# The recurrence's small levels on four column groups of TensorE, with compact diagonal blocks

## The chip, the cores and the metric

The kernel runs on one core of a Trainium2 chip. The metric is the device time of one execution in microseconds; the time before is the median of three runs.

## The reference

One layer of a streaming encoder for 1024 prompt tokens and 64 sample tokens (T = 1088), model width 1024, in fp32. One input projection feeds eight heads of forgetting attention and four heads (128 wide) of a gated linear recurrence, both gated, joined, and mapped by one output projection. The part that matters here is the recurrence, S_t = diag(f_t) S_{t-1} + k_t v_t^T, o_t = S_t^T q_t, in chunks:

```python
b = jnp.cumsum(logf, axis=1)
o_inter = jnp.einsum('blhk,bhkv->blhv', q * jnp.exp(b), S0)
diff = b[:, :, None] - b[:, None, :]
decay = jnp.exp(jnp.where(causal[None, :, :, None, None], diff, -jnp.inf))
A = jnp.einsum('bthk,btshk,bshk->bhts', q, decay, k)
o = o_inter + jnp.einsum('bhts,bshv->bthv', A, v)
b_last = b[:, -1]
S_new = jnp.exp(b_last)[..., None] * S0 + jnp.einsum('bshk,bshv->bhkv', jnp.exp(b_last[:, None] - b) * k, v)
```

The decay sits inside the sum over k, so A is no plain product of q and k.

## The kernel before

The work falls into four stages: loading and splitting x and the weights, with the projection of the attention's values; the attention with the projections of its keys and queries as filler; from about 340 us on the recurrence, whose four heads are interleaved with the remaining projections and with the first half of the output projection; and the rest of the output projection with the final norm, from about 640 us on.

Projections are split in three fp32r products (high by high, low by high, high by low). `t_block` (L248) gives 128 output columns for 364, 364 and 360 tokens, 24 matmuls each, into one of two `pj` banks of PSUM; DVE and ACT read the bank out (L1060, L1061 and the like).

**A head of the recurrence** (`hgrn_head`, L1092 on) computes A without cumulative sums, in a binary tree over chunks of 128 tokens (`NT` = 8, and the 64 sample tokens as a ninth). At level b a block of 2b tokens has an upper half of keys and a lower half of queries; the keys k are scaled up to the block's middle and the queries q from there, and their product is the block's b x b corner of A. `update(b)` then scales k, q1 and the products of forget values F on DVE for the next level. Level 0 is the diagonal (a sum over k by a product with `ones`, L1146 and L1147). Levels 1 and 2 share one product (queries copied to `qx`), levels 4 and 8 another (copied to `qy`, where level 8 takes two masks). Up to level 16 a product takes all 128 keys of a chunk as the stationary side and the lower-half queries of the chunk as the moving side (`pe.matmul(out, stationary, moving)`): L1166, L1227 and, through `level_mm`, L1105. Only a few small blocks of each 128-row result are wanted. `copy_predicated` on DVE puts these into `AT` (128 keys x 9 chunks x 128 queries) under the constant `masks`. The sample's products are half as large and go to a bank of their own (`psm`: L1147, L1179, L1239, L1108), with masked copies of their own (L1119, L1180, L1182, L1241).

Level 32 already uses 32 keys as the stationary side (L1260), with the outputs of a chunk's two halves on PSUM partitions 0 to 31 and 64 to 95, hence two column groups of 32. Level 64 uses 64 keys, all outputs on partitions 0 to 63 (L1273, copied to AT by L1275). Then k is transposed to `kn` (L1287), the states S of the chunks are made (L1306, L1318), and the outputs are AT and the state times values and q1 (L1335, L1337), normed to `og`. `post_stream` transposes `og` (L1362) and gates it into `mixH`. These products are all fp32; every fp32 matmul of the code is two matmul records in the trace.

**Order.** `Order.run` writes the instructions of three streams (recurrence, output transposes, projections) in an order set by a planner's clock. A stream's `yield (a, b)` adds a ns to the clock, as TensorE time, and says that its next step is due b ns later; `yield ("ev", ...)` waits for a named event. While a level's result goes through DVE (`LAT`: 4200 ns a level), the projections fill TensorE. A scheduler that knows the tiles then places instructions within each engine, so program order can shift somewhat.

Of the kernel before, what the change touches and what calls it, by code (L numbers as in the profile page):

```python
# [15 lines left out]
P = 128  # L16
# [52 lines left out]
def tile_fox_hgrn2(  # L69
# [337 lines left out]
    with tc.tile_pool(name="start", bufs=2, side="right") as sp:  # L407
# [170 lines left out]
        masks = ct([P, 7, 64], U8, "masks")  # L578
# [12 lines left out]
        dve.tensor_copy(masks[:], mtmp[:])  # L591
# [424 lines left out]
    with ExitStack() as hctx:  # L1016
# [4 lines left out]
        pool.memset(AT[:], 0.0)  # L1021
        ones = hp.tile([P, P], F32, tag="ones", name="ones")
# [70 lines left out]
        def hgrn_head(h):  # L1093
# [9 lines left out]
            def level_mm(pb, psm, sm0, kk, qv, npair, w):  # L1103
                for n in range(NT):
                    pe.matmul(pb[:, n * 64:(n + 1) * 64], kk[:, chunk_cols(n)],  # L1105
                              qv[:, n * npair:(n + 1) * npair, w, :], start=True, stop=True)
                np2 = npair // 2
                pe.matmul(psm[:DEC, sm0:sm0 + 32], kk[:, SEQ:T],  # L1108
                          qv[:, NT * npair:NT * npair + np2, w, :], start=True, stop=True)

            def level_put(pb, psm, sm0, ml, b, w):
                atv = at[:, 0:NT, :].rearrange("s n (c w o) -> s n c w o", w=2, o=b)[:, :, :, w, :]
                mk = masks[:, ml, :].rearrange("s (c o) -> s c o", o=b)
                dve.copy_predicated(
                    atv, mk.unsqueeze(1).broadcast_to([P, NT, 64 // b, b]),
                    pb[:].rearrange("s (n c o) -> s n c o", c=64 // b, o=b))
                ats = at[:DEC, NT, :DEC].rearrange("s (c w o) -> s c w o", w=2, o=b)[:, :, w, :]
                mk = masks[:DEC, ml, 0:32].rearrange("s (c o) -> s c o", o=b)
                dve.copy_predicated(ats, mk,  # L1119
                                    psm[:DEC, sm0:sm0 + 32].rearrange("s (c o) -> s c o", o=b))  # L1120
# [5 lines left out]
            def update(b, F, n=T):  # L1126
# [15 lines left out]
            psm = bank("tp")  # L1142
# [3 lines left out]
            pe.matmul(pb[:], ones[:], kq[:, 0:512], start=True, stop=True)  # L1146
            pe.matmul(psm[:DEC, 0:32], ones[:, :DEC], kq[:, 512:544], start=True, stop=True)  # L1147
            level_put(pb, psm, 0, 0, 1, 0)
# [4 lines left out]
            qxv = qx[:, 0:SEQ].rearrange("k (n w t) -> k n w t", w=2, t=64)  # L1153
            qsv = qx[:, SEQ:T].rearrange("k (w t) -> k w t", w=2)
            q2v = views(2)[0]
            act.copy(qxv[:, :, 0, :], q[:, 0:SEQ].rearrange("k (n t w) -> k n t w", t=64, w=2)[:, :, :, 1])
            act.copy(qsv[:, 0, :], qraw[:, 512:544, 1, 0])
            act.copy(qxv[:, :, 1, :].rearrange("k n (c o) -> k n c o", o=2),
                     q1[:, 0:SEQ].rearrange("k (n c w o) -> k n c w o", c=32, w=2, o=2)[:, :, :, 1, :])
            act.copy(qsv[:, 1, :].rearrange("k (c o) -> k c o", o=2), q2v[:, 256:272, 1, :])  # L1160
            yield (900.0, LAT["lvl0"])
            for g in range(2):
                pb = bank("st")
                for n in range(4):
                    c = chunk_cols(4 * g + n)
                    pe.matmul(pb[:, n * P:(n + 1) * P], k[:, c], qx[:, c], start=True, stop=True)  # L1166
                pv = pb[:].rearrange("s (n w t) -> s n w t", w=2, t=64)
                a4 = at[:, 4 * g:4 * g + 4, :]
                dve.copy_predicated(a4.rearrange("s n (t w) -> s n t w", w=2)[:, :, :, 1],
                                    masks[:, 1, :].unsqueeze(1).broadcast_to([P, 4, 64]),  # L1170
                                    pv[:, :, 0, :])
                dve.copy_predicated(
                    a4.rearrange("s n (c w o) -> s n c w o", w=2, o=2)[:, :, :, 1, :],
                    masks[:, 2, :].rearrange("s (c o) -> s c o", o=2)
                    .unsqueeze(1).broadcast_to([P, 4, 32, 2]),
                    pv[:, :, 1, :].rearrange("s n (c o) -> s n c o", o=2))
                yield (860.0, 0.0)
            psm = bank("tp")
            pe.matmul(psm[:DEC, 32:96], k[:, SEQ:T], qx[:, SEQ:T], start=True, stop=True)  # L1179
            dve.copy_predicated(at[:DEC, NT, :DEC].rearrange("s (t w) -> s t w", w=2)[:, :, 1],  # L1180
                                masks[:DEC, 1, 0:32], psm[:DEC, 32:64])
            dve.copy_predicated(  # L1182
                at[:DEC, NT, :DEC].rearrange("s (c w o) -> s c w o", w=2, o=2)[:, :, 1, :],
                masks[:DEC, 2, 0:32].rearrange("s (c o) -> s c o", o=2),
                psm[:DEC, 64:96].rearrange("s (c o) -> s c o", o=2))
            F = update(2, F)
            yield (100.0, LAT["lvl"])
# [5 lines left out]

            def part(i, a, b):

                return qy[i][:, 0:768].rearrange("k (n s c o) -> k n s c o", n=4, s=3, o=b)[:, :, a]

            def spart(a, b):
                return qy[1][:, 768 + 32 * a:800 + 32 * a].rearrange("k (c o) -> k c o", o=b)
# [7 lines left out]
            for i in range(2):  # L1207
                act.copy(part(i, 0, 4), q4[:, 64 * i:64 * i + 64, 1, :].rearrange("k (n c) o -> k n c o", n=4))
            act.copy(spart(0, 4), q4[:, 128:136, 1, :])
# [3 lines left out]
            for i in range(2):  # L1213
                src = q8[:, 32 * i:32 * i + 32, 1, :].rearrange("k (n c) o -> k n c o", n=4)
                act.copy(part(i, 1, 8), src)
                dve.tensor_tensor(part(i, 2, 8), src,
                                    F4s[:, 32 * i:32 * i + 32, :].rearrange("k (n c) o -> k n c o", n=4)
                                    .broadcast_to([P, 4, 8, 8]), op=ALU.mult)
            act.copy(spart(1, 8), q8[:, 64:68, 1, :])
            dve.tensor_tensor(spart(2, 8), q8[:, 64:68, 1, :], F4s[:, 64:68, :].broadcast_to([P, 4, 8]),  # L1220
                                op=ALU.mult)
            yield (0.0, LAT["qy"])
            for g in range(4):
                pb = bank("st")
                i = g // 2
                for n in range(2):
                    pe.matmul(pb[:, n * 192:(n + 1) * 192], k[:, chunk_cols(2 * g + n)],  # L1227
                              qy[i][:, (2 * (g % 2) + n) * 192:(2 * (g % 2) + n + 1) * 192],
                              start=True, stop=True)
                pv = pb[:, 0:384].rearrange("s (n w t) -> s n w t", n=2, t=64)  # L1230
                for a, b in ((0, 4), (1, 8), (2, 8)):
                    dve.copy_predicated(
                        at[:, 2 * g:2 * g + 2, :].rearrange("s n (c w o) -> s n c w o", w=2, o=b)[:, :, :, 1, :],
                        masks[:, 3 + a, :].rearrange("s (c o) -> s c o", o=b)
                        .unsqueeze(1).broadcast_to([P, 2, 64 // b, b]),
                        pv[:, :, a, :].rearrange("s n (c o) -> s n c o", o=b))
                yield (640.0, 0.0)
            psm = bank("tp")
            pe.matmul(psm[:DEC, 0:96], k[:, SEQ:T], qy[1][:, 768:864], start=True, stop=True)  # L1239
            for a, b in ((0, 4), (1, 8), (2, 8)):  # L1240
                dve.copy_predicated(  # L1241
                    at[:DEC, NT, :DEC].rearrange("s (c w o) -> s c w o", w=2, o=b)[:, :, 1, :],
                    masks[:DEC, 3 + a, 0:32].rearrange("s (c o) -> s c o", o=b),
                    psm[:DEC, 32 * a:32 * a + 32].rearrange("s (c o) -> s c o", o=b))
# [3 lines left out]
            yield (160.0, LAT["lvl"])  # L1248
            pb = bank("st")
            psm = bank("tp")  # L1250
            level_mm(pb, psm, 0, k, views(16)[0], 4, 1)
            level_put(pb, psm, 0, 6, 16, 1)
            F = update(16, F)
            yield (1000.0, LAT["lvl"])
# [14 lines left out]

            pb = bank("st")  # L1270
            for n in range(NT):
                t0 = n * P
                pe.matmul(pb[0:64, n * 64:(n + 1) * 64], k[:, t0:t0 + 64], q1[:, t0 + 64:t0 + P],  # L1273
                          start=True, stop=True)
            dve.tensor_copy(at[0:64, 0:NT, 64:P], pb[0:64, :].rearrange("s (n t) -> s n t", t=64))  # L1275
            F = update(64, F, SEQ)
            yield (900.0, LAT["lvl"])


            kn = h2.tile([P, NT + 1, P], F32, tag="kn", name=nm("kn"), bufs=1)  # L1280
            for g in range(3):
# [354 lines left out]
```

## Time and profile before

| | |
|---|---|
| median of 3 runs | 713.12 us (712.42 to 713.15) |
| profiled execution, its own time | 713.66 us |
| its span | 711.9 us |
| TensorE busy | 697.8 us (98%), granted clock 0.997 |
| weight loads busy | 628.4 us |
| DVE, ACT, POOL busy | 445.8, 319.2, 152.2 us |
| mean DMA rate | 72 GB/s |

The span is the time from the first to the last instruction of the program on the core. Busy times are unions over an engine's instructions. Consecutive matmuls overlap in the records: the duration of a record has a fixed part of about 0.2 us, so cost is read from starts, not from durations. A row of the timeline merges records of one line: start, length to the end of the last, engine, line, operation, output and inputs, columns and rows, the moving shape, and the count.

### The profile page before, as it was taken

The page shows a single profiled execution, that of the slowest core. Times are in us where ns is not written, and L with a number is a line of the kernel's source. Part 1 is how long each engine was busy: PE and PEld are TensorE (multiplying, and loading weights), DVE is VectorE, ACT ScalarE, POOL GpSimd, SP SyncE. Part 2 cuts the span into 40 slices and gives each one's busy share as a digit, 9 for nine tenths or more (in the row PEclk, how much of TensorE's full clock was granted, in tenths as well). Part 3 has the DMA queues.
Part 4 walks back from the last instruction along what each step waited for, and adds up shares of the span by engine and source line. Part 5 has one row for each costly group of instructions (what it writes and reads, how often), then busy time and mean ns, then how long its engine had stood idle before and what let it go on. Part 6 is the DMA issues. An engine that isn't in the chain of part 4 may idle for free.

```text
span 711.9 us, 11891 instructions
## 1 busy us (share of the span) xinstructions
PE 697.8 (98%) x4256; PEld 628.4 (88%) x4256; DVE 445.8 (63%) x1131; ACT 319.2 (45%) x822; POOL 152.2 (21%) x216
## 2 busy tenths in 40 slices
PE   9999999999999999999999999999999999999996
PEld 7889989888898897789999999999999998878885
DVE  4545368666667746754984674645975689753542
ACT  6755553655558456665412331332313324413542
POOL 4044932442424215110000100010000100012422
PEclk9999999999999999999999999999999999999998
DMA  8923322222232213112202110110111103341211
GB/s 309 336 69 114 95 75 57 57 53 61 57 86 31 50 21 105 18 31 90 60 1 64 37 32 1 64 39 30 33 52 40 37 31 128 117 137 55 95 44 60
DMA packets 40711, 51.10 MB, mean 72 GB/s; under 512 B 22870, under 2 KB 25766, under 8 KB 40652
## 3 DMA queue, kind: packets, MB, share of 16 engines
q1 hardware_dynamic: 40476, 50.25, 23.4%
q8 instruction: 34, 0.56, 0.3%
q14 instruction: 25, 0.20, 0.1%
q10 hardware_dynamic: 176, 0.09, 0.1%
HBM read 36.32 MB, written 9.56 MB: 64 GB/s over the span
## 4 chain that ended last, share of the span: by engine, by line
PE 70%; DVE 1%; ACT 1%; issue 0%; POOLq 0%; DVEq 0%; POOL 0%; ACTq 0%
PE pj L248 30%; PE pj L1415 13%; PE pj L229 6%; PE av L865 4%; PE st L840 2%; PE st L1227 2%; PE st L841 1%; PE st L1306 1%; PE tp L793 1%; PE pj L1409 1%; PE st L1166 1%; PE st L1105 1%; PE st L1273 1%; PE av L1362 1%; PE pj L221 1%; PE tp L1335 1%
## 5 line engine op out<-in xcount | busy, mean ns | idle before, releaser
L248 PE MATMUL pj<-hT,whi 128*128 128x364 f32 (+1 forms) x1152 | 219.4, 330 | 0.0
L248 PEld LDWEIGHTS pj<-hT,whi 128*128 128x128 f32 x1152 | 194.3, 188 | 6.8 <-issue 0.5
L248 PE MATMUL pj<-hT,wlo 128*128 128x364 f32 (+1 forms) x576 | 116.6, 333 | 0.0
L248 PEld LDWEIGHTS pj<-hT,wlo 128*128 128x128 f32 x576 | 96.7, 188 | 3.4 <-issue 0.5
L846 ACT ACTIVATE ph<-st 128x512 fp32r<-128x512 f32 (+1 forms) x96 | 46.9, 488 | 65.4 <-DVE st L843 42.7
L848 DVE TENSOR_TENSOR pl<-st,ph 128x512 fp32r<-128x512 f32 (+1 forms) x96 | 53.0, 553 | 30.9 <-ACT st L847 30.3
L109 POOL TENSOR_SCALAR rr<-ss 128x4 f32<-128x4 f32 (+1 forms) x12 | 2.3, 190 | 280.1 <-ACT og L1341 279.9
L1415 PE MATMUL pj<-hT,mx 128*128 128x512 f32 (+1 forms) x264 | 56.3, 374 | 0.0
L1415 PEld LDWEIGHTS pj<-hT,mx 128*128 128x128 f32 x264 | 46.2, 188 | 10.0
L175 POOL TENSOR_TENSOR wlo<-wr,whi 128x256 fp32r<-128x256 f32 (+1 forms) x52 | 36.8, 737 | 75.0 <-ACT ph L846 39.1
L174 ACT ACTIVATE whi<-wr 128x256 fp32r<-128x256 f32 (+1 forms) x112 | 38.2, 407 | 28.7 <-PE pj L248 16.9
L847 ACT ACTIVATE st<-st 128x512 f32<-128x512 f32 (+1 forms) x96 | 46.5, 485 | 0.0
L840 PE MATMUL st<-QX,KX 128*128 128x512 f32 (+1 forms) x96 | 34.9, 364 | 2.8 <-DVE pl L848 2.5
L229 PE MATMUL pj<-whi,hT 128*128 128x264 f32 (+1 forms) x256 | 36.6, 285 | 0.1
L1415 PE MATMUL pj<-hT,mxp 128*128 128x512 f32 x144 | 36.4, 403 | 0.0
L865 PE MATMUL av<-ph,VH 128*128 128x512 f32 (+1 forms) x96 | 33.4, 348 | 1.9 <-ACT ph L846 1.9
L229 PEld LDWEIGHTS pj<-whi,hT 128*128 128x128 f32 x256 | 33.8, 188 | 1.4 <-DVE q L1062 0.3
L841 PE MATMUL st<-QY,KY 68*128 68x512 f32 (+3 forms) x96 | 33.4, 348 | 0.6 <-issue 0.6
L865 PE MATMUL av<-pl,VH 128*128 128x512 f32 (+1 forms) x96 | 33.0, 344 | 0.0
L1061 ACT ACTIVATE sq<-pj 128x364 f32<-128x364 f32 (+1 forms) x21 | 9.9, 472 | 50.9 <-DVE pj L1060 50.9
L865 PE MATMUL av<-ph,VL 128*64 128x512 f32 (+1 forms) x96 | 32.4, 337 | 0.0
L793 PE MATMUL tp<-KY,QY 66*128 66x128 f32 (+5 forms) x96 | 32.2, 351 | 0.0
(307 smaller groups left out, 1288.6 us busy)
## 6 DMA issues: line engine op xcount, KB each, us to landing
wr<-in_w_t_dram SPq DMA_DIRECT2D x24, 512.0 KB
x<-in_xT_dram SPq DMA_DIRECT2D x16, 272.0 KB
xn<-in_x_prompt_dram SPq DMA_DIRECT2D x8, 512.0 KB
wo_raw<-in_w_out_dram SPq DMA_DIRECT2D x8, 512.0 KB
yp<-in_x_prompt_dram SPq DMA_DIRECT2D x6, 512.0 KB
out_dram<-yp SPq DMA_DIRECT2D x12, 256.0 KB
out_dram<-kT SPq DMA_DIRECT2D x4, 544.0 KB
wv<-in_w_v_dram SPq DMA_DIRECT2D x8, 256.0 KB
```

The lines of the kernel that those rows point to most:

```text
L174: act.activation(hf[:, cs], raw[:, cs], AF.Copy)
L175: self.eng.tensor_tensor(lf[:, cs], raw[:, cs], f32(hf[:, cs]), op=ALU.subtract)
L229: pe.matmul(pb[:rows, :width], a[:, j, t0:t0 + rows], w[j // 4][b][:, j % 4, :], start=(g == 0 and j == 0), stop=(g == 2 and j == 7))
L248: pe.matmul(pb[:, :n], w[:, j, :], h[:, j, t0:t0 + n], start=(g == 0 and j == 0), stop=(g == 2 and j == 7))
L793: pe.matmul(pb[:, :n], qy[rows, qs], ky[rows, k0:k0 + n], start=True, stop=True)
L840: pe.matmul(st[:, :n], kx[:, ks], qx[:, qs], start=True, stop=False)
L841: pe.matmul(st[:, :n], ky[YM[s], ks], qy[YM[s], qs], start=False, stop=True)
L846: act.activation(ph[:, :n], st[:, :n], AF.Exp)
L847: act.activation(st[:, :n], st[:, :n], AF.Exp)
L848: dve.tensor_tensor(pl[:, :n], st[:, :n], f32(ph[:, :n]), op=ALU.subtract)
L865: pe.matmul(av[mm, cols], w[:, b, :], x[:, :n], start=(b == 0 and w is VH[s] and x is ph), stop=(b == nblk - 1 and w is VL[s]), skip_group ...
L1415: pe.matmul(pb[:rows, :n], mx[:, a, j, :rows], wo[b][:, j0 + j, c0:c0 + n], start=(g == 0 and j == 0), stop=(g == 2 and j == nj - 1))
```

## The change

- Levels 0 to 16 no longer form a chunk's full 128-row product. `level_mm` forms, for each of the 34 blocks of 32 tokens, the block's 32 keys by its own lower-half queries (32 columns for levels 1 and 2 together, 48 for levels 4 and 8, 16 for level 16). The four blocks of a chunk go to PSUM partitions 0, 32, 64 and 96, so to four column groups. The sample has two blocks; they are computed twice, so that a ninth chunk of four is full. Level 0 is split in the same way.
- The results of these levels go to a new tile `AD` (128 x 9 x 32), which holds each chunk's four 32 x 32 diagonal blocks side by side: one masked copy for each mask, with the sample in it. `masks` shrinks from 64 to 16 columns. After level 16, four ACT copies put AD's blocks on the diagonal of AT.
- Level 64 uses the two halves of the array in turn, and half of its result is copied by ACT.
- The steps of levels 1, 2, 4 and 8 are issued in one piece each, and the planner's costs are changed.
- `state_hgrn` of a head is loaded ahead of the transposes of k, into a tenth buffer of `S`.
- The output transposes of heads 0 to 2 wait for all three outputs of the head; the ninth uses a `tp` bank.

```diff
-        masks = ct([P, 7, 64], U8, "masks")
+        masks = ct([P, 7, 16], U8, "masks")
...
-        dve.tensor_copy(masks[:], mtmp[:])
+        for a in range(4):
+            dve.tensor_copy(masks[a * 32:a * 32 + 32], mtmp[a * 32:a * 32 + 32, :, a * 16:a * 16 + 16])
...
+        AD = hp.tile([P, NT + 1, 32], F32, tag="AD", name="AD")
+        pool.memset(AD[:], 0.0)
...
+            def level_mm(pb, w, qv):
+                for n in range(NT + 1):
+                    for a in range(4):
+                        x = 4 * n + (a if n < NT else a % 2)
+                        pe.matmul(pb[32 * a:32 * a + 32, n * w:(n + 1) * w], k[:, 32 * x:32 * x + 32], qv(x),
+                                  start=True, stop=True)
+            def level_put(pv, ml, b, w):
+                adv = AD[:].rearrange("s n (c w o) -> s n c w o", w=2, o=b)[:, :, :, w, :]
+                mk = masks[:, ml, :].rearrange("s (c o) -> s c o", o=b)
+                dve.copy_predicated(adv, mk.unsqueeze(1).broadcast_to([P, NT + 1, 16 // b, b]),
+                                    pv.rearrange("s n (c o) -> s n c o", o=b))
...
-            pe.matmul(pb[:], ones[:], kq[:, 0:512], start=True, stop=True)
-            pe.matmul(psm[:DEC, 0:32], ones[:, :DEC], kq[:, 512:544], start=True, stop=True)
-            level_put(pb, psm, 0, 0, 1, 0)
+            for a in range(4):
+                kqa = kq[:, 0:512].rearrange("k (n a t) -> k a n t", a=4, t=16)[:, a]
+                pe.matmul(pb[32 * a:32 * a + 32, 0:128], ones[:, 0:32], kqa, start=True, stop=True)
+                t0 = 512 + 16 * (a % 2)
+                pe.matmul(pb[32 * a:32 * a + 32, 128:144], ones[:, 0:32], kq[:, t0:t0 + 16], start=True, stop=True)
+            level_put(pb[:, 0:144].rearrange("s (n t) -> s n t", t=16), 0, 1, 0)
...
-            for g in range(2):
-                pb = bank("st")
-                for n in range(4):
-                    c = chunk_cols(4 * g + n)
-                    pe.matmul(pb[:, n * P:(n + 1) * P], k[:, c], qx[:, c], start=True, stop=True)
...
-                yield (860.0, 0.0)
...
+            yield (300.0, LAT["lvl0"])
+            pb = bank("st")
+            level_mm(pb, 32, lambda x: qx[:, 32 * x:32 * x + 32])
+            pv = pb[:, 0:288].rearrange("s (n w t) -> s n w t", w=2, t=16)
+            level_put(pv[:, :, 0, :], 1, 1, 1)
+            level_put(pv[:, :, 1, :], 2, 2, 1)
             F = update(2, F)
-            yield (100.0, LAT["lvl"])
+            yield (900.0, LAT["lvl"])
...
-            for g in range(4):
...
-                yield (640.0, 0.0)
...
+            level_mm(pb, 48, lambda x: qy[x >= 16][:, (x - 16 * (x >= 16)) * 48:
+                                                  (x - 16 * (x >= 16)) * 48 + 48])
...
             F = update(8, F8)
-            yield (160.0, LAT["lvl"])
+            yield (1000.0, LAT["lvl"])
...
-            level_mm(pb, psm, 0, k, views(16)[0], 4, 1)
-            level_put(pb, psm, 0, 6, 16, 1)
+            q16 = views(16)[0]
+            level_mm(pb, 16, lambda x: q16[:, x, 1, :])
+            level_put(pb[:, 0:144].rearrange("s (n t) -> s n t", t=16), 6, 16, 1)
             F = update(16, F)
-            yield (1000.0, LAT["lvl"])
+            for a in range(4):
+                nn = NT + 1 if a < 2 else NT
+                ds = slice(32 * a, 32 * a + 32)
+                act.copy(at[ds, 0:nn, ds], AD[ds, 0:nn, :])
+            yield (700.0, LAT["lvl"])
...
-                t0 = n * P
-                pe.matmul(pb[0:64, n * 64:(n + 1) * 64], k[:, t0:t0 + 64], q1[:, t0 + 64:t0 + P],
+                t0, a, c0 = n * P, 64 * (n % 2), n // 2 * 64
+                pe.matmul(pb[a:a + 64, c0:c0 + 64], k[:, t0:t0 + 64], q1[:, t0 + 64:t0 + P],
                           start=True, stop=True)
-            dve.tensor_copy(at[0:64, 0:NT, 64:P], pb[0:64, :].rearrange("s (n t) -> s n t", t=64))
+            ato = at[0:64, 0:NT, 64:P].rearrange("s (n w) t -> s w n t", w=2)
+            dve.tensor_copy(ato[:, 0], pb[0:64, 0:256].rearrange("s (n t) -> s n t", t=64))
+            act.copy(ato[:, 1], pb[64:P, 0:256].rearrange("s (n t) -> s n t", t=64))
             F = update(64, F, SEQ)
-            yield (900.0, LAT["lvl"])
+            yield (600.0, LAT["lvl"])
+            s0 = h2.tile([P, P], F32, tag="S", name=nm("S"), bufs=10)
+            sync.dma_start(s0[:], state_hgrn[0, 0, h])
...
                 for g in range(3):
+                    if h < NG - 1:
+                        yield ("ev", "o", h, 2)
                     yield ("ev", "o", h, g)
...
-                    pt = bank("av")
+                    pt = bank("av" if g < 2 else "tp")
...
-                    yield (107.0 * nn, LAT["post"] if g == 1 else 0.0)
+                    yield (107.0 * nn, LAT["post"] if g == 1 and h == NG - 1 else 0.0)
```

The copies that fill `qx` and `qy` change their layout with it, and the sample's separate copies go.

More of the change, by code (lines that the diff above doesn't have):

```diff
@@ L1101, in chunk_cols @@
                 return slice(n * P, (n + 1) * P)
[L1103 to L1112, printed above, removed]
-                mk = masks[:, ml, :].rearrange("s (c o) -> s c o", o=b)
[L1114 to L1120, printed above, removed]
+            def level_mm(pb, w, qv):
[6 more added lines that the diff above has]
+                adv = AD[:].rearrange("s n (c w o) -> s n c w o", w=2, o=b)[:, :, :, w, :]
+                mk = masks[:, ml, :].rearrange("s (c o) -> s c o", o=b)
+                dve.copy_predicated(adv, mk.unsqueeze(1).broadcast_to([P, NT + 1, 16 // b, b]),
+                                    pv.rearrange("s n (c o) -> s n c o", o=b))
             def views(b, n=T):
@@ L1141, in hgrn_head @@
             pb = bank("st")
-            psm = bank("tp")
             kq = G("kq")
@@ L1152, in hgrn_head @@
             qx = G("qx")
[L1153 to L1159, printed above, removed]
@@ L1160, in hgrn_head @@
-            act.copy(qsv[:, 1, :].rearrange("k (c o) -> k c o", o=2), q2v[:, 256:272, 1, :])
-            yield (900.0, LAT["lvl0"])
-            for g in range(2):
-                pb = bank("st")
-                for n in range(4):
-                    c = chunk_cols(4 * g + n)
[L1166 to L1176, printed above, removed]
-                yield (860.0, 0.0)
@@ L1178, in hgrn_head @@
[L1178 to L1185, printed above, removed]
+            qxv = qx[:].rearrange("k (x w t) -> k x w t", w=2, t=16)
@@ new lines, in hgrn_head @@
+            act.copy(qxv[:, :, 0, :], q[:].rearrange("k (x t w) -> k x t w", t=16, w=2)[:, :, :, 1])
+            act.copy(qxv[:, :, 1, :].rearrange("k x (c o) -> k x c o", o=2),
+                     q1[:].rearrange("k (x c w o) -> k x c w o", c=8, w=2, o=2)[:, :, :, 1, :])
+            yield (300.0, LAT["lvl0"])
[3 more added lines that the diff above has]
+            level_put(pv[:, :, 0, :], 1, 1, 1)
@@ L1192, in hgrn_head @@
             qy = [G("qy") for _ in range(2)]
+            QN = (16, 18)
             def part(i, a, b):
-                return qy[i][:, 0:768].rearrange("k (n s c o) -> k n s c o", n=4, s=3, o=b)[:, :, a]
-            def spart(a, b):
-                return qy[1][:, 768 + 32 * a:800 + 32 * a].rearrange("k (c o) -> k c o", o=b)
+                return qy[i][:, 0:48 * QN[i]].rearrange("k (x s c o) -> k x s c o", s=3, c=16 // b, o=b)[:, :, a]
             F4 = F[:, 0:272].rearrange("k (c w) -> k c w", w=2)
@@ L1207, in hgrn_head @@
             for i in range(2):
-                act.copy(part(i, 0, 4), q4[:, 64 * i:64 * i + 64, 1, :].rearrange("k (n c) o -> k n c o", n=4))
-            act.copy(spart(0, 4), q4[:, 128:136, 1, :])
+                act.copy(part(i, 0, 4), q4[:, 64 * i:64 * i + 4 * QN[i], 1, :].rearrange("k (x c) o -> k x c o", c=4))
             dve.tensor_tensor(q4[:, :, 1, :], q4[:, :, 1, :], F4[:, :, 0:1].broadcast_to([P, 136, 4]),
@@ L1213, in hgrn_head @@
             for i in range(2):
-                src = q8[:, 32 * i:32 * i + 32, 1, :].rearrange("k (n c) o -> k n c o", n=4)
+                cs = slice(32 * i, 32 * i + 2 * QN[i])
+                src = q8[:, cs, 1, :].rearrange("k (x c) o -> k x c o", c=2)
                 act.copy(part(i, 1, 8), src)
                 dve.tensor_tensor(part(i, 2, 8), src,
-                                    F4s[:, 32 * i:32 * i + 32, :].rearrange("k (n c) o -> k n c o", n=4)
-                                    .broadcast_to([P, 4, 8, 8]), op=ALU.mult)
@@ L1219, in hgrn_head @@
-            act.copy(spart(1, 8), q8[:, 64:68, 1, :])
-            dve.tensor_tensor(spart(2, 8), q8[:, 64:68, 1, :], F4s[:, 64:68, :].broadcast_to([P, 4, 8]),
-                                op=ALU.mult)
-            yield (0.0, LAT["qy"])
-            for g in range(4):
[L1224 to L1236, printed above, removed]
-                yield (640.0, 0.0)
@@ L1238, in hgrn_head @@
-            psm = bank("tp")
-            pe.matmul(psm[:DEC, 0:96], k[:, SEQ:T], qy[1][:, 768:864], start=True, stop=True)
+                                  F4s[:, cs, :].rearrange("k (x c) o -> k x c o", c=2)
+                                  .broadcast_to([P, QN[i], 2, 8]), op=ALU.mult)
+            yield (0.0, LAT["qy"])
+            pb = bank("st")
+            level_mm(pb, 48, lambda x: qy[x >= 16][:, (x - 16 * (x >= 16)) * 48:
+                                                  (x - 16 * (x >= 16)) * 48 + 48])
@@ L1240, in hgrn_head @@
+            pv = pb[:, 0:432].rearrange("s (n w t) -> s n w t", w=3, t=16)
             for a, b in ((0, 4), (1, 8), (2, 8)):
[L1241 to L1244, printed above, removed]
+                level_put(pv[:, :, a, :], 3 + a, b, 1)
             dve.tensor_tensor(k4[:, :, 0, :], k4[:, :, 0, :], F4[:, :, 1:2].broadcast_to([P, 136, 4]),
@@ L1247, in hgrn_head @@
             F = update(8, F8)
-            yield (160.0, LAT["lvl"])
+            yield (1000.0, LAT["lvl"])
             pb = bank("st")
-            psm = bank("tp")
-            level_mm(pb, psm, 0, k, views(16)[0], 4, 1)
-            level_put(pb, psm, 0, 6, 16, 1)
+            q16 = views(16)[0]
+            level_mm(pb, 16, lambda x: q16[:, x, 1, :])
+            level_put(pb[:, 0:144].rearrange("s (n t) -> s n t", t=16), 6, 16, 1)
             F = update(16, F)
-            yield (1000.0, LAT["lvl"])
+            for a in range(4):
[3 more added lines that the diff above has]
+            yield (700.0, LAT["lvl"])
             pb = bank("st")
@@ L1307, in hgrn_head @@
                 if g == 2:
-                    s0 = h2.tile([P, P], F32, tag="S", name=nm("S"), bufs=9)
-                    sync.dma_start(s0[:], state_hgrn[0, 0, h])
                     S.append(s0)
@@ L1312, in hgrn_head @@
                     c = 4 * g + n
-                    S2 = h2.tile([P, P], F32, tag="S", name=nm("S"), bufs=9)
+                    S2 = h2.tile([P, P], F32, tag="S", name=nm("S"), bufs=10)
                     if S[-1] is None:
@@ L1333, in hgrn_head @@
                     cs = chunk_cols(n)
-                    s0 = S[c] if g < 2 else S[NT + 1]
-                    pe.matmul(po[:w, cs], AT[:w, c, :w], vv(g, n), start=True, stop=(s0 is None))
-                    if s0 is not None:
-                        pe.matmul(po[:w, cs], q1[:, t0:t0 + w], s0[:], start=False, stop=True)
+                    sc = S[c] if g < 2 else S[NT + 1]
+                    pe.matmul(po[:w, cs], AT[:w, c, :w], vv(g, n), start=True, stop=(sc is None))
+                    if sc is not None:
+                        pe.matmul(po[:w, cs], q1[:, t0:t0 + w], sc[:], start=False, stop=True)
                 ss = h2.tile([P, 4], F32, tag="ss4", name=nm("ss4"), bufs=3)
```

## The prediction

> **What bounds the kernel now.** I read the page's first part first, then its chain of waits, then the busy time by stage, and last the timeline of TensorE through one head of the recurrence, since that is where the change lies.
>
> ```profile
> PE 697.8 (98%) x4256; PEld 628.4 (88%) x4256; DVE 445.8 (63%) x1131; ACT 319.2 (45%) x822; POOL 152.2 (21%) x216
> ```
> ```profile
> PE 70%; DVE 1%; ACT 1%; issue 0%; POOLq 0%; DVEq 0%; POOL 0%; ACTq 0%
> ```
> ```profile
> 340.00:640.00 300.00, 299.83 (x2034) 279.46 (x2033) 210.09 (x514) 91.87 (x297) 12.54 (x24) 1.00 0.17 54
> 640.00:700.00 60.00, 60.00 (x261) 48.25 (x260) 26.50 (x68) 26.16 (x82) 19.00 (x32) 1.00 0.19 66
> ```
>
> TensorE is busy 98% of the span and the chain that ended last runs on it. The last two rows are stretches (start, end, length, then busy us of PE, weight loads, DVE, ACT, POOL, then the granted clock): in 340 to 640 us, which holds all four heads of the recurrence, PE has 0.17 us without a matmul, at clock 1.00, and the 60 us behind it have none. Nothing waits there but the queue for TensorE, so an instruction's time taken off TensorE in that stretch moves the end by as much, as long as projections are ready to fill the gaps. DVE (70% there) and ACT (31%) are covered.
>
> **How a fp32 product costs, and what a column group costs.** An fp32 matmul of the program appears as two records. I price a run of them from the start of its first record to the start of the next projection matmul (L248); where the run begins on fewer than 128 columns, a wait at its entry comes on top. The runs of the third head, which the change touches, in order (start us, length us, engine, line, count):
>
> ```profile
> 499.58 1.02 PE L1146 MATMUL st<-kq,ones 128*128 128x512 f32 x2
> 500.53 0.30 PE L1147 MATMUL tp<-kq,ones 128*64 128x32 f32 x2
> 500.76 1.59 PE L248 MATMUL pj<-hT,wlo 128*128 128x364 f32 x8
> ```
> Level 0: 500.76 - 499.58 = 1.18 us.
> ```profile
> 506.16 1.95 PE L1166 MATMUL st<-qx,k 128*128 128x128 f32 x16
> 508.04 0.33 PE L1179 MATMUL tp<-qx,k 128*64 128x64 f32 x2
> 508.30 2.93 PE L248 MATMUL pj<-hT,whi 128*128 128x360 f32 x16
> ```
> Levels 1 and 2: 2.14 us. A record here takes (1.95 - 0.275)/15 = 112 ns for 128 moving columns.
> ```profile
> 516.03 0.27 PE L1362 MATMUL av<-ident,og 64*128 64x64 f32 x1
> 516.23 1.57 PE L1227 MATMUL st<-qy,k 128*128 128x192 f32 x8
> 517.73 0.38 PE L1239 MATMUL tp<-qy,k 128*64 128x96 f32 x2
> 518.04 1.08 PE L248 MATMUL pj<-hT,wlo 128*128 128x364 f32 x5
> 518.96 1.46 PE L1227 MATMUL st<-qy,k 128*128 128x192 f32 x8
> 520.13 0.80 PE L248 MATMUL pj<-hT,wlo 128*128 128x364 f32 x3
> ```
> Levels 4 and 8: 1.81 + 1.17 = 2.98 us in two runs; a record of 192 columns takes about (1.46 - 0.33)/7 = 161 to 166 ns, so a column more costs some 0.83 ns.
> ```profile
> 524.08 1.89 PE L1105 MATMUL st<-q,k 128*128 128x64 f32 x16
> 525.90 0.30 PE L1108 MATMUL tp<-q,k 128*64 128x32 f32 x2
> 526.13 0.92 PE L248 MATMUL pj<-hT,wlo 128*128 128x360 f32 x4
> ```
> Level 16: 2.05 us. Half the columns of level 1 (64 against 128) bring nothing: 16 records last 1.89 us against 1.95. Below some width the load of the stationary side sets the pace.
> ```profile
> 529.54 1.49 PE L248 MATMUL pj<-hT,wlo 128*128 128x364 f32 x8
> 530.96 0.70 PE L1260 MATMUL st<-q,k 128*32 128x32 f32 x32
> 531.49 0.23 PE L1262 MATMUL st<-q,k 128*32 128x32 f32 x2
> 531.64 2.94 PE L248 MATMUL pj<-hT,whi 128*128 128x364 f32 x16
> ```
> Level 32 is not changed, and it is my price list: 32 keys by 32 queries, on two column groups in turn. 32 records (16 products) start within 0.70 - 0.20 = 0.50 us, so 16.3 ns a record. The two records of L1262 stand alone on one group and start 0.03 us apart (0.23 - 0.20). So one group needs about 32.5 ns a record, 65 ns a product, and two groups run side by side at full gain. The run costs 0.68 us; of that 0.52 and 0.065 are records, so about 0.10 is the way out, and the entry (the last L248 starts at 529.54 + 1.49 - 0.33 = 530.70, the next would have at 530.85) is 0.11. I take 0.20 us a run for going to narrow column tiles and back. The Trainium skill, TensorEngine Tiling, Key Properties, says that changing the tiling mode drains TensorE; these 0.10 us on each side agree, and the sum has them already.
> ```profile
> 536.51 1.15 PE L1273 MATMUL st<-q,k 128*64 128x64 f32 x16
> 537.59 2.26 PE L248 MATMUL pj<-hT,whi 128*128 128x364 f32 x12
> ```
> Level 64, all on one half of the array: 1.08 us and 0.10 at the entry; 58 ns a record ((1.15 - 0.22)/15 is 62, with the first one's start in it).
>
> Do groups overlap although a product's two records follow each other in the program? These rows of the sample attention say so:
> ```profile
> 105.62 0.27 PE L903 MATMUL tp<-pt,vs 64*64 64x64 f32 x1
> 105.63 0.27 PE L903 MATMUL tp<-pt,VH 64*64 64x64 f32 x1
> 105.73 0.22 PE L903 MATMUL tp<-pt,vs 64*64 64x64 f32 x1
> 105.73 0.22 PE L903 MATMUL tp<-pt,VH 64*64 64x64 f32 x1
> ```
> The code issues the product with vs, then that with VH, each two records; the trace starts vs, VH, vs, VH, the pairs within 0.01 us. Each column group goes on by itself. No row shows four groups. I take four as four independent groups of 65 ns a product, the value that two groups show without loss (16.3 is half of 32.5), and keep the two-group rate as the dear end.
>
> **The sum, per head.** New costs, four groups:
> - Levels 1 and 2: 8 + 1 products become 9 x 4 of 32 columns: 9 rounds x 65 ns = 0.59, with the switch 0.79 (was 2.14).
> - Levels 4 and 8: 9 x 4 of 48 columns; a record 32.5 + 16 x 0.83 = 46 ns; 9 x 92 = 0.83, with the switch 1.03 (was 2.98, two runs).
> - Level 16: 9 x 4 of 16 columns. By the lesson of level 16 above I give 16 columns no less than 32: 0.59 + 0.20 = 0.79 (was 2.05). If the pace did fall with the columns, 13 ns a record less, 0.23 us a head.
> - Level 0: on each group one product of 128 columns (2 x 112) and one of 16 (65): 0.29 + 0.20 = 0.49 (was 1.18).
> - Level 64: 8 products in turn on two halves: 8 x 117 / 2 = 0.47, with the switch 0.67 (was 1.18).
>
> Before 9.53, after 3.77: 5.76 us a head, 23.0 over four heads.
>
> The gathering of runs beside that:
> ```profile
> 511.72 1.04 PE L1362 MATMUL av<-ident,og 128*128 128x128 f32 x8
> 512.51 0.91 PE L248 MATMUL pj<-hT,wlo 128*128 128x364 f32 x4
> ```
> ```profile
> 542.31 1.04 PE L1287 MATMUL tp<-ident,k 128*128 128x128 f32 x8
> 543.18 0.27 PE L1287 MATMUL av<-ident,k 128*64 128x128 f32 x1
> 543.21 1.57 PE L248 MATMUL pj<-hT,whi 128*128 128x364 f32 x8
> ```
> The output transposes of heads 0 to 2 now wait for all three outputs and go as one run: 0.79 + 0.20 + 0.10 at the entry of the ninth (516.03) become what nine transposes cost in L1287, 0.90: 0.2 us a head for three heads, 0.5.
> ```profile
> 467.20 0.43 PE L1337 MATMUL st<-S,q 128*64 128x128 f32 x2
> 467.57 0.60 PE L248 MATMUL pj<-hT,wlo 128*128 128x360 f32 x2
> ```
> The sample's state product stands alone behind eight projections: 0.37 + 0.10. With state_hgrn loaded ahead of the kn transposes it may join the run before it, at 2 x 112 ns: 0.25 a head, 1.0 in all if it does, 0 if not; I take 0.5.
>
> Sum: 23.0 + 0.5 + 0.5 = 24.0 us. The profiled execution took 713.66 us, which gives 689.7; it lies 0.5 above the median of the three runs shown, so against 713.12 I say **689.2 us**.
>
> What is costed at nothing, and its cover:
> ```profile
> L1169 DVE COPY_PREDICATED AT<-masks,st x8: 721/755/809, 352.4 to 576.5; 128x256 f32<-128x256 uint8 x8
> ```
> ```profile
> L1208 ACT COPY qy<-q 128x256 f32<-128x256 f32 x8 | 2.8, 403 | 7.1 <-DVE q L1132 7.1
> ```
> - DVE: 25 masked copies a head become 7 of 144 elements, about 144/256 x 0.755 = 0.43 us each. DVE is off the path, so nothing is gained, but every level's result comes back sooner.
> - ACT: four copies of 32 x 288 from AD to AT, about 0.45 us each by L1208, and half of level 64's copy: some 2.1 us a head more; the separate small copies for the sample fall away. ACT has 208 of 300 us free. Queued behind the four copies are the sigmoids of the next projection (L1061), which free its bank; PE has two such banks and 24 matmuls of 0.152 us between, so 1.8 us fit. If that cover is gone: 4 x 1.8 = 7.2 us.
> - AD's memset on POOL and four mask copies instead of one run once, far ahead of the recurrence.
> - The load of state_hgrn moves on SP's queue ahead of the transposes; with ten buffers its slot is the previous head's load, long read, so what stands behind it (the next weight block) isn't held. POOL's queue is passed by nothing.
> - A shorter head needs more filler per level only if the planner asks for it; its latencies are the same. Behind the last head 48 projection matmuls are still left over:
> ```profile
> 630.37 11.51 PE L1415 MATMUL pj<-hT,mxp 128*128 128x512 f32 x48
> ```
> so the filler doesn't run out before the recurrence is through.
>
> **The rivals.**
> - *Two groups' pace is the limit* (the issue of records, or the array). With at least 16.3 ns a record, each of the three bursts is 72 x 16.3 = 1.17 + 0.20; a head saves 9.53 - (3 x 1.37 + 0.49 + 0.67) = 4.26, in all 18.0: 695.2. If at most two groups overlap, the 48-column burst is 36 x 46 = 1.66 + 0.20, and 697.1 follows. For it: no row shows a denser run. Against it: two groups lose nothing against one.
> - *A floor on starts of 25 ns.* If no two records could start closer than 25 ns, a burst would be 72 x 25 = 1.8 + 0.2, level 0 0.6: a head saves 9.53 - 7.27 = 2.26, in all 10.0, 703.1. L1260's 16.3 ns and L903's pairs speak against it. The Trainium skill, TensorE: Matmul & The Clock Gate, Part 1 ("Wait — 56ns, not 53.3ns?"), states such a floor of about 25 ns however small the width; the trace does not agree.
> - *A wait takes the gain back*: the ACT copies hold the next bank, 7.2 us at most: 696.4. Against it: ACT's idle.
> - *Slower: the four groups run one behind another.* 36 products in a row at 65, 92 and 65 ns are 2.34, 3.31 and 2.34, each + 0.20, level 0 4 x 0.29 + 0.20 = 1.36, level 64 1.18: 11.1 against 9.53, 6.4 us more in four heads, less the 1.0 of gathering: 718.5. The products got smaller and four times as many, so it turns at an overlap of about 1.15. Against it: level 32 and L903 overlap twofold.
> - *Nothing changes*: only if the runs are hidden now. 299.83 of 300 us speaks against it.
>
> **How the numbers follow.** Four groups side by side 0.62 (own range 685 to 693: below, by 0.9 for 16 columns, 0.5 for the state product and half of the switches' cost, 0.1 x 5 x 4 = 2.0; above, by the ACT copies' half). Two groups' pace 0.22, ACT's wait 0.07, the floor 0.02, serial groups 0.05, no change 0.02. The range 685 to 699 takes in the first two and part of the third, above 8 in 10. What can be told from no change here is about 0.2%, 1.4 us: faster 0.92, same 0.02, slower 0.06.
>
> **What would show it.** Right: in the changed profile the three bursts of a head are one run each of 72 records with some 0.6, 0.8 and 0.6 us between first and last start (8 to 9 ns a record, 11 to 12 for the 48 columns), and level 64's 16 records within 0.5 us; PE still without idle in the stretch of the recurrence; DVE's busy time down by some 20 us or more, ACT's up by a few. Wrong: bursts of 1.2 us or more (two groups), or a PE idle row released by ACT's copy of AT, or projections' L248 rows that grow longer between the runs.

## The result, and the profile after

| | before | after |
|---|---|---|
| median | 713.13 us | 689.41 us |
| lowest to highest | 712.42 to 715.41 | 688.99 to 689.69 |
| profiled execution, its span | 713.66, 711.9 | 689.64, 687.9 |
| ratio to before, 95% interval | | 0.9662 (0.9639 to 0.9684) |

The forecast was 689.2 us (685 to 699). Three executions of the experiments ran far slower than the others of their kernel (2368 us in experiment 3; 757 and 1615 us the first time in experiment 6) and are left out of all medians. The first part of the profile's page and its chain, after:

```profile
PE 674.5 (98%) x4952; PEld 608.4 (88%) x4952; DVE 423.0 (61%) x1058; ACT 325.2 (47%) x826; POOL 152.2 (22%) x217
...
PE 67%; DVE 1%; DMA 1%; SPq 1%; POOL 1%; ACT 1%; issue 0%; POOLq 0%; DVEq 0%; ACTq 0%
```

TensorE runs 696 more records in 23.3 us less, is as full as before, and still carries the chain. DVE's busy time fell by 22.8 us, ACT's rose by 6.0. By stage, the recurrence with its projections (start, end, length, busy us of PE, weight loads, DVE, ACT, POOL with the number of instructions, granted clock, DMA share and GB/s):

```profile
330.00:620.00 290.00, 289.89 (x2808) 272.01 (x2808) 192.15 (x449) 105.45 (x313) 14.03 (x27) 1.00 0.20 61
```

PE again has next to no idle, 0.11 us. From the first record of level 0 to the first record of the final output rows it takes 273.3 us, before 297.1: 23.8 of the span's 24.0 us come from this stage. The timeline of the third head, the runs that answer to those of before (rows as before: start, length to the last end):

```profile
487.81 0.45 PE L1148 MATMUL st<-kq,ones 128*32 128x128 f32 x8
488.05 0.25 PE L1150 MATMUL st<-kq,ones 128*32 128x16 f32 x8
488.23 1.60 PE L248 MATMUL pj<-hT,wlo 128*128 128x364 f32 x8
489.67 2.80 PE L248 MATMUL pj<-hT,whi 128*128 128x364 f32 x16
492.31 1.48 PE L248 MATMUL pj<-hT,wlo 128*128 128x360 f32 x8
493.72 0.83 PE L1114 MATMUL st<-qx,k 128*32 128x32 f32 x72
494.48 2.93 PE L248 MATMUL pj<-hT,whi 128*128 128x360 f32 x16
...
497.91 1.04 PE L1330 MATMUL av<-ident,og 128*128 128x128 f32 x8
498.88 0.27 PE L1330 MATMUL tp<-ident,og 64*128 64x64 f32 x1
499.08 0.93 PE L248 MATMUL pj<-hT,wlo 128*128 128x364 f32 x4
...
503.28 0.97 PE L1114 MATMUL st<-qy,k 128*32 128x48 f32 x72
504.19 0.94 PE L248 MATMUL pj<-hT,wlo 128*128 128x364 f32 x4
...
509.02 0.80 PE L1114 MATMUL st<-q,k 128*32 128x16 f32 x72
509.75 2.92 PE L248 MATMUL pj<-hT,whi 128*128 128x360 f32 x16
...
514.61 0.70 PE L1224 MATMUL st<-q,k 128*32 128x32 f32 x32
515.14 0.23 PE L1226 MATMUL st<-q,k 128*32 128x32 f32 x2
515.30 2.26 PE L248 MATMUL pj<-hT,whi 128*128 128x364 f32 x12
...
520.15 0.69 PE L1237 MATMUL st<-q,k 128*64 128x64 f32 x16
520.77 1.58 PE L248 MATMUL pj<-hT,whi 128*128 128x360 f32 x8
...
536.02 0.43 PE L1303 MATMUL st<-S,q 128*64 128x128 f32 x2
536.39 1.58 PE L248 MATMUL pj<-hT,whi 128*128 128x364 f32 x8
```

Each row of 72 records lasts 0.8 to 1.0 us in all. A record lasts about 0.2 us, so the starts are (0.83 - 0.20)/71 = 8.9 ns apart at 32 columns; at 16 they are 8.7 ns apart, at 48 10.8. A group's own records are four times that apart, about 35 and 43 ns. Half the columns bring next to nothing below 32, as level 16 of before had said.

### The profile page after: what moved, and what is told of

The parts are those of the page before. It is cut to its first block, busy times and chain, and to the rows that moved or that the text cites. A ratio compares the mean times of both kernels' runs of the same rounds, so it can differ in the third digit from the quotient of the medians.

```text
span 687.9 us, 13216 instructions
## 1 busy us (share of the span) xinstructions
PE 674.5 (98%) x4952; PEld 608.4 (88%) x4952; DVE 423.0 (61%) x1058; ACT 325.2 (47%) x826; POOL 152.2 (22%) x217
## 4 chain that ended last, share of the span: by engine, by line
PE 67%; DVE 1%; DMA 1%; SPq 1%; POOL 1%; ACT 1%; issue 0%; POOLq 0%; DVEq 0%; ACTq 0%
PE pj L248 30%; PE pj L1383 13%; PE pj L229 7%; PE av L867 4%; PE st L842 2%; PE st L1114 1%; PE st L843 1%; PE st L1274 1%; PE pj L1377 1%; PE tp L795 1%; SPq L780 1%; DMA wr<-in_w_t_dram 1%; PE tp L1301 1%; PE av L1301 1%; PE tp L1303 1%; PE tp L1255 1%
## 5 line engine op out<-in xcount | busy, mean ns | idle before, releaser
L1383 PEld LDWEIGHTS pj<-hT,mxp 128*128 128x128 f32 x144 | 26.4, 188 | 6.3 <-ACT mxp L1370 0.3
```

The source lines that it names most:

```text
L1383: pe.matmul(pb[:rows, :n], mx[:, a, j, :rows], wo[b][:, j0 + j, c0:c0 + n], start=(g == 0 and j == 0), stop=(g == 2 and j == nj - 1))
```

## The experiments

All times are medians; the kernel before ran in the same rounds (713.3, 713.9 and 712.9 us in the three sets), and ratios are to it, with a 95% interval.

**1. The order of the products: group by group.**
```diff
-                for n in range(NT + 1):
-                    for a in range(4):
+                for a in range(4):
+                    for n in range(NT + 1):
```


> The changed kernel with the products of levels 1 to 16 issued group by group (all nine of column group 0, then all nine of group 1, and so on) instead of chunk by chunk. Same instructions, same results. Theory (the gain comes from four column groups running side by side, and they do so only when their products stand close together in the program): the three bursts of a head go from 0.83, 0.97 and 0.80 us to about 36 x 65 ns = 2.3, 36 x 92 = 3.3 and 2.3 us, so 5.6 us more a head, 22 us in all: about 712 us, nearly the whole gain lost. Rival (the gain comes from the smaller products as such, or TensorE looks far enough ahead to overlap groups anyway): 689.4, bursts unchanged; with a look-ahead of about ten products something between, near 700.

Measured: 707.12 us, ratio 0.991 (0.989 to 0.993). The timeline of the third head:
```profile
502.46 2.17 PE L1114 MATMUL st<-qx,k 128*32 128x32 f32 x72
504.56 2.92 PE L248 MATMUL pj<-hT,whi 128*128 128x360 f32 x16
...
513.36 2.83 PE L1114 MATMUL st<-qy,k 128*32 128x48 f32 x72
516.11 0.93 PE L248 MATMUL pj<-hT,wlo 128*128 128x364 f32 x4
```
From the first start to the next projection, the same 72 records take 2.10 and 2.75 us in place of 0.76 and 0.91. Narrower products alone therefore bring next to nothing: levels 1 and 2 cost 2.14 us as full products. 17.7 of the 23.7 us hang on the order alone. Of the 6.0 us that remain, levels 0 and 64, whose order this edit leaves as it was, hold 4.6 (0.67 and 0.47 us a head, by the runs priced below). The theory said 712; the measured time is 5 us less. Within a group the single records start 31 to 32 ns apart (42 to 43 at 48 columns); 72 of 32 ns would be 2.30 us, and without the 0.10 of the way out it is 2.00. So each of the three borders between groups saves about 0.1 us: some three records of the next group start before the last ones of the group ahead of them in the program.

**2. Two groups at a time.**
```diff
-                for n in range(NT + 1):
-                    for a in range(4):
+                for a0 in (0, 2):
+                  for n in range(NT + 1):
+                    for a in (a0, a0 + 1):
```


> The changed kernel with the products of levels 1 to 16 issued for column groups 0 and 1 over all chunks, then for groups 2 and 3. Theory (each group goes on at about 32 to 35 ns a record by itself): two side by side give 16.3 ns a record at 32 and 16 columns and 23 at 48, bursts of about 1.2, 1.7 and 1.2 us, 1.7 us more a head: 696 us. Rival (what limits a burst is the rate at which TensorE starts records, 9 ns each, whatever their group): bursts unchanged, 689.4.

Measured: 694.64 us, ratio 0.974 (0.972 to 0.976).
```profile
495.67 1.24 PE L1115 MATMUL st<-qx,k 128*32 128x32 f32 x72
...
505.63 1.59 PE L1115 MATMUL st<-qy,k 128*32 128x48 f32 x72
...
511.98 1.23 PE L1115 MATMUL st<-q,k 128*32 128x16 f32 x72
```
(1.24 - 0.20)/71 = 14.6 ns a record, 19.5 at 48 columns: two groups' pace, a little better again by the border in the middle. The pace follows the number of groups at work; it is not a fixed rate at which records start. This also decides the prediction's main rival, two groups' pace as the limit: 695.2 us was its time, and two groups at a time take 694.64.

**3. The gathering alone.**
```diff
-                yield (860.0, 0.0)
...
-                yield (640.0, 0.0)
...
+            s0 = h2.tile([P, P], F32, tag="S", name=nm("S"), bufs=10)
+            sync.dma_start(s0[:], state_hgrn[0, 0, h])
...
+                    if h < NG - 1:
+                        yield ("ev", "o", h, 2)
```
(on the kernel before, the products unchanged; the planner's cost of a level stands at its end)

> The kernel before with the gathering alone: levels 1 and 2, and 4 and 8, issued in one piece each, the state loaded ahead of the transposes of k, the output transposes of heads 0 to 2 in one run. The products stay full 128-row products. Theory: of the 23.7 us the gathering is worth at most 1: 712.0 to 713.1. Rival (the gain is in the number of switches between fp32 runs and projections): ten runs fewer should bring several us, below 710.

Measured: 712.80 us, ratio 0.9992 (0.9981 to 1.0004): nothing that can be told from no change. The rival, several us from fewer switches, falls.

**4. DVE's relief.** DVE's busy time fell by 22.8 us, and I had costed that at nothing. To put it back without touching TensorE:
```diff
+                for _ in range(4):
                     dve.copy_predicated(adv, mk.unsqueeze(1).broadcast_to([P, NT + 1, 16 // b, b]),
                                         pv.rearrange("s n (c o) -> s n c o", o=b))
```


> The changed kernel with each masked copy of a level's result issued four times (the same result): 21 copies more a head, about 0.4 us each, 34 us more of DVE, so DVE is busier than in the kernel before. Theory (DVE is off the path; its relief brings nothing): 689.4 within 0.7; at most 1 us more if the projections' matmuls, whose mean distance fell from 170.6 to 169.5 ns, gained from DVE's relief. Rival (part of the gain is DVE's relief, through results that come back sooner): several us more, 693 or above, with idle of PE that DVE releases.

Measured: 692.15 us, ratio 0.971 (0.968 to 0.973), so 2.7 us more: above the theory's 0.7 and below the rival's 693, though the four executions scatter from 690.7 to 694.4. DVE's busy time rose by 20.8 us to 443.8, to that of before (445.8) and not above it. The list of PE's waits named the place (who waited for whom, us, times, longest):
```profile
PE pj L1384 <- DVE yp L1414: 1.3, 1, 1.3
PE pj L1384 <- DVE hgt L1067: 0.3, 1, 0.3
```
Both lie at 575 to 581 us, in the last head, where DVE also splits the output weights and adds up the first output rows. To tell place from amount, the copies were repeated in the first three heads alone, and in the last alone (`range(4 if h < NG - 1 else 1)` and `range(4 if h == NG - 1 else 1)`).

> The masked copies four times in the first three heads only (the same result). With four times in all heads the time rose by 2.7 us, and its trace has 1.6 us of PE idle behind DVE, all in the last head, where DVE also splits the output weights. Theory (DVE has room in the first three heads, and none in the last one's hand-over to the output projection): 689.4 within 0.7. Rival (the extra DVE work costs everywhere, in proportion): three quarters of 2.7, 691.4.

> The masked copies four times in the last head only (the same result). Theory: all of the 2.7 us, 691.5 to 692.2, with PE idle behind DVE between the last head's levels 16 and 64. Rival (in proportion): a quarter, 690.1.

Measured: 689.08 us (ratio 0.966, 0.964 to 0.969) and 691.99 us (0.970, 0.968 to 0.972). 16.4 us more of DVE's busy time in three heads cost nothing, 4.3 us in the last cost all 2.7. By stage, the kernel with the copies in the first three heads, then the one with them in the last:
```profile
330.00:550.00 220.00, 219.91 (x2196) 212.25 (x2195) 155.94 (x385) 79.68 (x229) 10.28 (x21) 1.00 0.16 47
550.00:620.00 70.00, 69.98 (x613) 59.66 (x613) 51.97 (x128) 25.82 (x84) 3.13 (x6) 1.00 0.34 105
```
```profile
330.00:550.00 220.00, 219.91 (x2195) 212.26 (x2194) 139.56 (x322) 79.64 (x229) 10.54 (x21) 1.00 0.16 47
550.00:620.00 70.00, 68.27 (x597) 57.79 (x597) 56.14 (x147) 26.29 (x84) 3.12 (x6) 0.98 0.33 105
```
```profile
581.63 1.16 PE L1384 MATMUL pj<-hT,mxp 128*128 128x512 f32 x4 [1.61 <-DVE yp L1414]
...
582.90 1.12 PE L1238 MATMUL st<-q,k 128*64 128x64 f32 x16
```
```profile
582.00:585.00 3.00, 3.00 (x24) 2.25 (x23) 3.00 (x9) 1.18 (x3) 0.00 (x0) 0.64 0.99 386
585.00:590.00 5.00, 5.00 (x22) 3.98 (x21) 3.22 (x7) 0.61 (x3) 0.00 (x0) 0.87 0.14 57
```
With DVE at 156 of 220 us PE has next to no idle; with 56 of 70 it has 1.7 us, 1.6 of it in one wait for the addition that empties its bank (L1414). The wait is only half of the price in this profile: behind it the granted clock is 0.64 for 3 us and 0.87 for 5 us, and level 64's run takes 1.12 us there in place of 0.69. By the clock that is an estimated 0.36 x 3 + 0.13 x 5 = 1.7 us, and 1.6 + 1.7 is the 3.3 us between this execution (692.92) and the changed kernel's profiled one (689.64). With the copies in all heads, the profiled execution (690.72, the fastest of its four) has the waits of 0.3 and 1.3 us and a clock of 1.00 behind them. Why the clock fell in one and not in the other, and what it was in the executions without a trace, is not shown.

So the relief brought no time, but in the last head it was needed to keep what the groups gave.

**5. How far ahead a group reaches.** Experiment 1 left the depth open. Two, then three products in a row for each group:
```diff
+                for n0 in range(0, NT + 1, 2):   # 3 in the second
+                  for a in range(4):
+                    for n in range(n0, min(n0 + 2, NT + 1)):
```


> The changed kernel with the products of levels 1 to 16 issued two in a row for each column group (chunks 0 and 1 on group 0, the same on group 1, and so on). Theory (each group takes about 3 to 4 records ahead, as the overlap at the borders between groups in the group-by-group order shows; the issue stops when a group's place is full): two products are four records, which nearly fit: bursts as in the changed kernel, 0.83 and 0.97 us, up to 0.2 more: 689.4 to 691. Rival (records of four groups overlap only if the very next product is on another group): two in a row halve the overlap, bursts near 1.2, 1.6 and 1.2 us: 694.5.

> The same with three products in a row for each column group. Theory (3 to 4 records ahead): of six records two to three wait for the group, 64 to 96 ns at each of 12 borders, 24 records in 0.26 to 0.38 us: 11 to 16 ns a record, bursts about 1.0 to 1.3 us at 32 and 16 columns and 1.3 to 1.6 at 48: 692 to 695. Rival (a look-ahead of a dozen products): unchanged, 689.4. Rival (no look-ahead): about 1.6 to 2.2, 698 to 700.

Measured: 690.37 us (ratio 0.967, 0.965 to 0.969) and 696.36 us (0.975, 0.974 to 0.977). First levels 1 and 2, 4 and 8, 16 with two in a row, then with three:
```profile
493.50 0.92 PE L1115 MATMUL st<-qx,k 128*32 128x32 f32 x72
...
503.11 1.07 PE L1115 MATMUL st<-qy,k 128*32 128x48 f32 x72
...
508.94 0.89 PE L1115 MATMUL st<-q,k 128*32 128x16 f32 x72
```
```profile
497.04 1.36 PE L1115 MATMUL st<-qx,k 128*32 128x32 f32 x72
...
507.13 1.71 PE L1115 MATMUL st<-qy,k 128*32 128x48 f32 x72
...
513.61 1.35 PE L1115 MATMUL st<-q,k 128*32 128x16 f32 x72
```
Two in a row, four records, cost only 0.1 us a burst (a level's 72 records). Three in a row lose 0.5 to 0.7 us, and the time lies above the forecast's 692 to 695. An estimate from these runs: issue in program order, let each group have one record at work for 32 ns and room for two more, and stop the issue at a record that finds no room. Counted through, one, two, three and nine products in a row then take 0.54, 0.64, 1.22 and 1.98 us from first to last start, and the pairs of experiment 2 take 1.02; the rows have 0.63, 0.72, 1.16, 1.97 and 1.04. With room for one more, two in a row would take 1.12; with room for three more, three in a row would take 0.86. So a reach of about three records a group fits all five orders within 0.1 us, where three to four was expected; a look-ahead of a dozen products, or none, doesn't fit.

**6. A version that goes further.** What the runs of the timeline leave: level 32 is on two groups, and the sample's products of 64 rows have switches of their own.
```diff
-                    t0 = n * P + a
-                    pe.matmul(pb[a:a + 32, n * 32:(n + 1) * 32], k[:, t0:t0 + 32],
+                    t0, o, c0 = n * P + a, a + 32 * (n % 2), n // 2 * 32
+                    pe.matmul(pb[o:o + 32, c0:c0 + 32], k[:, t0:t0 + 32],
...
+            pool.memset(kn[DEC:P, NT, :], 0.0)
...
+                if g == 2:
+                    pool.memset(og[DEC:P, 0, :], 0.0)
...
-                        pe.transpose(pt[:, n * P:n * P + w], og[:w, n, :], ident[:w, :w])
+                        pe.transpose(pt[:, n * P:(n + 1) * P], og[:, n, :], ident[:])
```
(and half of level 32's result copied by ACT, the sample's values in a tile of 128 rows with zeros below, its products over 128 rows)

> The changed kernel with level 32 on four column groups too (even chunks on groups 0 and 2, odd ones on 1 and 3, half of its result copied by ACT), and the sample's products with 128 contraction rows in place of 64 (kn, the values and og padded with zero rows). Theory (TensorE time is all that counts; a run's switch to other tile sizes costs about 0.1 us a side): level 32 from 0.77 to about 0.50 us a head, the ninth output transpose from 0.3 to 0.1, the sample's state and output products from about 1.1 to 0.8: 0.8 us a head, 3 us in all, 686.4. Rival (overheads this small disappear in the projections around them, as the gathering's did): level 32's 1.0 alone, 688.4, or nothing, 689.4.

> The changed kernel as it is, on the same chip and in the same rounds, for the small differences of the other three: 689.4.

> The version with level 32 on four groups and the sample's products with full rows once more, for an undisturbed profile: 686.1, with level 32's run near 0.5 us and one run's ninth output transpose at about 0.1 us.

Measured: 685.67 us beside 689.34 for the changed kernel in the same rounds, ratios 0.960 (0.959 to 0.962) and 0.966 (0.964 to 0.968); in the third set of rounds 686.07, ratio 0.962 (0.960 to 0.964). In the profile of that second time:
```profile
496.51 1.04 PE L1335 MATMUL av<-ident,og 128*128 128x128 f32 x8
497.38 0.27 PE L1335 MATMUL tp<-ident,og 128*128 128x128 f32 x1
497.41 0.91 PE L248 MATMUL pj<-hT,wlo 128*128 128x364 f32 x4
...
512.93 0.46 PE L1225 MATMUL st<-q,k 128*32 128x32 f32 x32
513.20 0.23 PE L1227 MATMUL st<-q,k 128*32 128x32 f32 x2
513.36 2.26 PE L248 MATMUL pj<-hT,whi 128*128 128x364 f32 x12
```
Level 32's run falls from 515.30 - 514.61 = 0.69 us to 0.43. The ninth transpose starts 0.03 us ahead of the projections instead of 0.20, and the run of nine takes 0.90 us instead of 1.17. The gain is 3.3 to 3.7 us where 3 were forecast, more than level 32's 1.0 us, so the rival falls.

## Why the prediction was right

- **TensorE is the bound**: right. 0.11 us without a matmul in 290 us; what the runs lost, the span lost (22.6 us of its 24.0, below).
- **Four groups as four independent groups**: right, and shown by experiments 1 and 2 rather than by the time alone. The prediction took it from two groups. The price of a group's record, by itself in experiment 1, was right at 32 columns (32 ns) and too high at 48 (43 for 46). With four groups at work the group's record takes about 35 ns at 32 columns, so four together lose a tenth where the prediction had no loss: 0.06 us a run.
- **The runs**, third head, from first start to the next projection with 0.09 us for the entry (0.11 in the prediction, which took the projections as 0.15 us apart; these rows have 2.64/16 = 0.165), forecast in brackets: level 0 0.51 (0.49), levels 1 and 2 0.85 (0.79), 4 and 8 1.00 (1.03), 16 0.82 (0.79), 64 0.71 (0.67). Together 3.89 for 3.77, 5.64 us a head for 5.76: 22.6 us for 23.0.
- **The gathering of the transposes, 0.5 us**: wrong; this term brought nothing. The run of nine costs 499.08 - 497.91 = 1.17 us, no less than the runs it replaces (1.09). I took nine transposes at L1287's price of 0.90, but the ninth here has 64 rows, and the way in and out of that tile costs nearly 0.3 us wherever it stands. Experiment 3 found nothing for the gathering as a whole, and experiment 6 removed that cost with zero rows.
- **The sample's state product, 0.5**: near by luck. It joined the run before it in all four heads, which was priced at 1.0; but it still costs 536.39 - 536.02 = 0.37 in place of 0.47, so 0.10 a head where 0.25 was taken: 0.4 over four heads.
- **What was costed at nothing**: the masked copies took 0.32 us (I had 0.43), the copies to AT 0.41 (0.45), and neither held PE (no wait of PE is listed from 330 to 640 us):
```profile
L1120 DVE COPY_PREDICATED AD<-masks,st x28: 302/319/491, 345.3 to 571.9; 128x144 f32<-128x144 uint8 x28
L1217 ACT COPY AT<-AD x16: 402/410/434, 366.4 to 573.9; 32x288 f32<-32x288 f32 x8, 32x256 f32<-32x256 f32 x8
```
  "DVE is off the path, so nothing is gained" held for the gain. It hid a condition: with 4.3 us of DVE work put back in the last head, 2.7 us of the gain went. The prediction's reserve of left-over projections didn't cover that.
- **The rest**: 22.6 + 0.4 is 23.0 of the stage's 23.8 us. The other 0.8 us lie between the runs, and the sum had no term for them. Behind a run of other products, the second projection starts 0.27 us after the first; elsewhere projections start 0.17 us apart (means over the stage: 266 and 166 ns, before and after alike). In the rows above, the eight projections from 488.23 take 1.44 us, where eight at the pace of the sixteen behind them would take 1.32. The trace has 35 such places before and 27 after, because runs were joined: eight times 0.1 us. A price that ends at the first projection's start leaves this out. On average the projections of 364 columns now start 169.5 ns apart instead of 170.6; DVE's relief isn't the cause, since with the copies repeated they stay at 169.5. That the forecast, with 0.5 us too much for the transposes and 0.4 too much for the runs, still came out within 0.2 us is luck: this 0.8 us made up for them.

## What to carry to other kernels

Small fp32 products on TensorE pay by the column groups that work at once, and the order of issue decides that: walk the groups in the inner loop, with at most two products in a row on one. Price a run from first start to the next full-width start, switches included, from rows of the same kernel, and look at the start after that as well, since it came 0.1 us late here behind every run. Then ask of every engine that you relieve whether the new pace would have needed the relief.

## What the runs showed of the hardware

- Records of different column groups pass each other: at a border between groups, some three records of the next group start before the last ones of the group ahead of them in the program (experiment 1, 2.00 us for 2.30). A reach of about three records a group fits the five orders of experiments 1, 2 and 5; this is an estimate, since no row shows the queue itself.
- With four groups, records start 8.7 to 8.9 ns apart at 16 and at 32 columns, 10.8 at 48. Part 1 of the Trainium skill's page TensorE: Matmul & The Clock Gate ("Wait — 56ns, not 53.3ns?") states a floor of about 25 ns; the measurement decides against it for column groups.
- A transpose of 64 contraction rows behind full ones costs nearly 0.3 us for the switches (1.17 us for the run of nine, 0.90 with zero rows).
- Behind a run of other products, the second projection starts 0.27 us after the first, elsewhere 0.17.
- Behind a wait of 1.6 us the granted clock was 0.64 for 3 us and 0.87 for 5 us; behind one of 1.3 us, in another execution, it stayed at 1.00.
